# Two vector subtracts moved to GpSimd and a split copy moved to ScalarE in a two-layer diffusion backbone

## The chip, the cores and the metric

The kernel runs on one core of a Trainium2 chip. The metric is device time in microseconds (us) of one execution; lower is better. The engines are named as in the profile: PE is TensorE (PEld its weight loads), DVE is VectorE, ACT is ScalarE, POOL is GpSimd and SP is SyncE, which here only issues transfers.

## The reference, cut to what matters

Two layers work on 512 latent and 256 context tokens of width 1024. All arithmetic is fp32.

```python
for l in range(DEPTH):                                    # DEPTH = 2
    mod = split(silu_c @ w_mod[l] + b_mod[l], 6)          # shift, scale, gate, twice
    p = split_proj((layer_norm(x) * (1 + scale) + shift) @ w_in[l] + b_in[l])
    y_r, y_a, y_m = retention(p), attention(p), mlstm(p)  # three token mixers
    z = sig(g_r) * (y_r @ w_r) + sig(g_a) * (y_a @ w_a) + sig(g_m) * (y_m @ w_m)
    x = layer_norm(alpha * x + mod[2] * (z @ w_o)) * ln1_g + ln1_b
    h = layer_norm(x) * (1 + mod[4]) + mod[3]
    u = depthwise_conv3(h @ w_up[l]) + conv_b[l]
    a, g = split(u, 2)
    x = layer_norm(alpha * x + mod[5] * ((silu(g) * a) @ w_down[l])) * ln2_g + ln2_b
```

The context stream goes through the same steps, except that it is not carried beyond the mixers in the second layer.

## The kernel before, in words

**Split products.** An fp32 matrix product is made of three reduced-precision ones. Each operand is split into a high half (the value rounded to fp32r) and a low half (the value less the high half), and high times high, high times low and low times high are added up in PSUM. So each weight and each activation needs a cast (high half) and a subtract (low half) before PE can use it.

**Weights.** All weights stream from HBM once, mostly in blocks of 128x1024 words. `wblock` (L308) loads a block into `raw` (five buffers, issued by SP), casts it to `wh` on ACT (L313, two buffers) and subtracts to `wl` on DVE (L314, two buffers). There are 358 such blocks. `fm` (L432) uses a block as the stationary operand against the transposed activations `xh` and `xl`; `tm` (L447) uses it as the moving operand. Both first run all products with `wh` and then those with `wl`, so `wl` is needed later than `wh`. Some blocks of the last down-projection are kept for several passes and are split by code of their own (`keep`), with the subtract on DVE.

**Activations.** `to_xT` (L409) takes one token tile of 128 rows that is already normalised, transposes it on PE into PSUM in two halves of 512 columns, copies each 128x128 piece out with the scale and shift of the modulation into `mod`, casts that to `xh` on ACT (L425) and subtracts to `xl` on DVE (L426). The scaled copies of one half run on DVE (L421) and those of the other half on ACT (L423), turn about by tile. There are 88 copies on each engine.

**Layer boundaries.** `finish` (L1049) closes each sub-layer tile by tile: statistics, a power for the reciprocal deviation on POOL (L398), two DVE passes over the tile (L1070, L1071), a square with row sums on ACT (L1080), a second power on POOL (L1083), the bias `nb` on DVE (L1084), the normalised tile `xn` on ACT (L1086), and then `to_xT`. The layer norm at the start (L1031) also ends in `to_xT`.

**Merge operand.** `yprep` (L1294) reads the mixers' outputs back from DRAM into `stg`, casts to `xh` on ACT (L1299) and subtracts to `xl` on DVE (L1300), four pieces for each of two mixers and each layer.

**What sets the order.** The order of PE's instructions is written by hand: a `Mixer` interleaves a foreground generator (projections, merge, FFN) with background ones (mixers, `finish`), by an estimated running time. Every other engine runs in the order that the tile scheduler chose from its own simulation at build time. `wblock` raises the priority of its cast and subtract. Each engine runs its list strictly in order, so an instruction that waits holds back all that stand behind it.

Of the kernel before, what the change touches and what calls it, by code (L numbers as in the profile page):

```python
# [9 lines left out]
F32 = mybir.dt.float32  # L10
F32R = mybir.dt.float32r
BF = mybir.dt.bfloat16
AF = mybir.ActivationFunctionType
OP = mybir.AluOpType
# [189 lines left out]
def _program(es, nc, tc, I, OUT):  # L204
    V, S, G, SP = nc.vector, nc.scalar, nc.gpsimd, nc.sync
# [10 lines left out]
    def tr(out, in_):  # L216
        M.cost(0.107)
        nc.tensor.transpose(out, in_, ident)  # L218
# [12 lines left out]
    def Ht(name="h", dt=F32):  # L231
        return sp.tile([128, 512], dt, name=name, tag="H", bufs=12)
# [4 lines left out]
    def stg(name="stg"):  # L237
        return wp.tile([128, 768], F32, name=name, tag="stg", bufs=3)
# [4 lines left out]
    def pt(name="p"):  # L243
        return psp.tile([128, 512], F32, name=name, tag="p")
# [57 lines left out]
    def wload(src, n=1024):  # L302
        raw = wp.tile([128, 1024], F32, name="raw", tag="raw", bufs=5)
        with tc.high_priority():
            M.wdma = SP.dma_start(out=raw[:, :n], in_=src)
        return raw

    def wblock(src, n=1024):  # L308
        raw = wload(src, n)
        h = wp.tile([128, 1024], F32R, name="wh", tag="wh", bufs=2)  # L310
        l = wp.tile([128, 1024], F32R, name="wl", tag="wl", bufs=2)
        with tc.high_priority():
            S.copy(h[:, :n], raw[:, :n])  # L313
            V.tensor_tensor(l[:, :n], raw[:, :n], h[:, :n].bitcast(F32), op=OP.subtract)  # L314
        return h, l

    mod_tail = []
# [91 lines left out]
    def to_xT(xn, t, xh, xl, mc, sidx, s, hfs=(0, 1)):  # L409
        cols = slice(128 * t, 128 * t + 128)  # L410
        for hf in hfs:
            p = pt("ptr")
            for k in range(4):
                tr(p[:, 128 * k:128 * k + 128], xn[hf][:, 128 * k:128 * k + 128])
            m = Ht("mod")
            for k in range(4):
                kk = 4 * hf + k
                o, i = m[:, 128 * k:128 * k + 128], p[:, 128 * k:128 * k + 128]
                a, b = mc[:, sidx + 1, kk, s:s + 1], mc[:, sidx, kk, s:s + 1]
                if (hf + t) % 2 == 0:  # L420
                    V.tensor_scalar(o, i, a, b, op0=OP.mult, op1=OP.add)  # L421
                else:
                    S.activation(o, i, AF.Identity, scale=a, bias=b)  # L423
            m3 = m.rearrange("p (k t) -> p k t", k=4)
            S.copy(xh[:, 4 * hf:4 * hf + 4, cols], m3)  # L425
            M.xl = V.tensor_tensor(xl[:, 4 * hf:4 * hf + 4, cols], m3, xh[:, 4 * hf:4 * hf + 4, cols].bitcast(F32),  # L426
                                   op=OP.subtract)

    def new_xT():
        return (xp.tile([128, 8, 768], F32R, name="xh", tag="xh"), xp.tile([128, 8, 768], F32R, name="xl", tag="xl"))  # L430
# [16 lines left out]
    def tm(srcs, lhs, tiles, nks, evac, hook=None, w=256):  # L447
        per = 512 // w
        banks = [tiles[i:i + per] for i in range(0, len(tiles), per)]
        gs = [None] * len(banks)  # L450
        tot = sum(nks)
        done = 0
        for src, nk in zip(srcs, nks):
            h, l = src() if callable(src) else wblock(src, nk * w)
            for bi, ts in enumerate(banks):
                if hook:
                    yield from hook(int(done > 0), ts)
                if done == 0:
                    gs[bi] = gt()
                for i, t in enumerate(ts):  # L460
                    for k, pi in [(k, pi) for k in range(nk) for pi in (0, 1)] + [(k, 2) for k in range(nk)]:
                        mm(gs[bi][:, w * i:w * i + w], lhs(done + k, t, pi == 1), (l if pi == 2 else h)[:, w * k:w * k + w],
                           start=(done + k == 0 and pi == 0 and i == 0),
                           stop=(done + k == tot - 1 and pi == 2), skip_group_check=True)
                    yield
                if done + nk == tot:
                    evac(ts, gs[bi][:, :w * len(ts)].rearrange("p (t c) -> p t c", c=w))
            done += nk
# [546 lines left out]
    def start_x(xh, xl):  # L1015
# [22 lines left out]
        for hf in range(2):  # L1038
            if hf:
                yield "mods"  # L1040
            for t in order:
                to_xT(xts[t], t, xh, xl, modc[0], 0, int(t >= 4), (hf,))
                M.done.add(f"x0.0.{t}.{hf}")
                if not hf and t == 4:
                    load(3)
                    norm(3)
                yield 0 if hf else 0.5

    def finish(key, X, xslot, gname, bname, l, tiles, emit, xT=None, mc=None, sidx=0, mi=None):  # L1049
# [3 lines left out]
        def post(t, xn):  # L1053
            need_mod(*mi[:2])
            tmod(*mi[2:])
            to_xT(xn, t, xT[0], xT[1], mc, sidx, int(t >= 4))
            M.done.add(f"{key}.{t}")
# [55 lines left out]
    def layer(l, xT, key):  # L1113
        last = l == DEPTH - 1
        nq = 512 if last else 768
# [104 lines left out]
        for i in range(2):  # L1220
            t = km_[i]
            km.append(t)
            if i:
                gl = []
                for a, b in ALL:
                    p = pt("pgl")
                    for c in range(a, b, 128):
                        tr(p[:, c - a:c - a + 128], glt[:, c:c + 128])
                    gl.append((p[:, :b - a], a, b))
                M.add(mlstm(l, mlstm_rows(gl, bfm), qm, km, vm, chunks, nq))  # L1230
            yield from fm(wblock(I["wfm"][l, B_KM - 1 + i]), xh, xl, ALL,
                          lambda g, a, b: evac_bias(t[:, a:b], g, bq[:, B_KM + i:B_KM + i + 1], scale=0.125))
        for i in range(2):
            t = qm_[i]
            qm.append(t)
            yield from fm(wblock(I["wfm"][l, B_QM - 1 + i]), xh, xl, qseg,
                          lambda g, a, b: evac_bias(t[:, a:b], g, bfm[:, B_QM + i:B_QM + i + 1]))
# [54 lines left out]
        yh, yl = new_xT()  # L1292

        def yprep(bi):  # L1294
            for k in range(4):
                t = stg()
                kk = 4 * (bi % 2) + k
                SP.dma_start(out=t[:, :nq].rearrange("p (c t) -> p c t", t=128), in_=dr_y[bi][:, :nqt, k, :])
                S.copy(yh[:, kk, :nq], t[:, :nq])  # L1299
                V.tensor_tensor(yl[:, kk, :nq], t[:, :nq], yh[:, kk, :nq].bitcast(F32), op=OP.subtract)  # L1300

        def yatt(t, y):
            c = slice(128 * t, 128 * t + 128)
# [23 lines left out]
        def merge(bi, segs):  # L1327
# [3 lines left out]
            for q in range(4):  # L1331
                blk = wblock(I["wbr"][l, bi, q])
                if bi == 0 and q == 1:
                    yprep(1)
# [37 lines left out]
        yold = []  # L1372
        yield f"r{l}"
        yprep(0)
        tmod(0, 4, 4)
        yield from merge(0, qseg)
# [38 lines left out]
        for gr, (go, gnum) in enumerate(zip(GOFF, GROUPS)):  # L1415
# [4 lines left out]
            for pi, segs in enumerate(passes):  # L1420
# [3 lines left out]
                for jn, j in enumerate(range(go, go + gnum)):  # L1424
# [3 lines left out]
                    for half, jj in enumerate((j, NF + j)):  # L1428
                        t = stg("tc")
# [92 lines left out]
```

## Time and profile before

| what | value |
|---|---|
| median of 3 runs | 2539.36 us (2532.22 to 2539.62) |
| the profiled execution: its own time | 2537.32 us |
| its span, first to last instruction | 2535.4 us |
| granted PE clock, mean | 0.987 |
| PE busy | 2430.9 us (96%) |
| DVE busy | 1585.1 us (63%) |
| ACT busy | 1003.1 us (40%) |
| POOL busy | 92.2 us (4%) |

The engines run side by side, so busy times don't add up to the span. A PE that is busy 96% of the time leaves about 104 us of the span in which no matmul ran; the stretches in which these lie are where the other engines matter. The granted clock is the PE clock as a share of full speed: at 1.00 a stretch ran at the upper of two levels (2.4 GHz), at 0.5 at the lower (1.2 GHz), and a mean between them says how much of the stretch was spent at each.

### The profile page before, as it was taken

How to read it: one execution, taken by the hardware profiler on the slowest of the kernel's cores; microseconds unless marked ns; L12 is line 12 of the kernel's file. 1: busy time of each engine (PE TensorE's matmuls, PEld its weight loads, DVE VectorE, ACT ScalarE, POOL GpSimd, SP SyncE). 2: the span in 40 equal slices, each digit the busy share in tenths (PEclk: the TensorE clock that was granted, in tenths of full speed). 3: DMA queues.
4: the chain of work that ended last, by engine and by line, in shares of the span. 5: the costliest groups of instructions: out<-in, count | busy, mean ns of one | idle time of the engine just before them, and what ended most of it. 6: DMA issues, size and time to landing. Idle time of an engine off the chain costs nothing. (4 is left out here: it accounts for less than half of the span.)

```text
span 2535.4 us, 41733 instructions
## 1 busy us (share of the span) xinstructions
PE 2430.9 (96%) x16552; PEld 2147.9 (85%) x16552; DVE 1585.1 (63%) x3338; ACT 1003.1 (40%) x1802; POOL 92.2 (4%) x111
## 2 busy tenths in 40 slices
PE   6999999999899989999999989999999988999998
PEld 4977998888788978999898878779787888988887
DVE  5556465545576885555545773767565877865557
ACT  4423322455433463232313353334254555633332
POOL 1000001000000000000000010000110000000000
PEclk9999999999999999999999999999999999999999
DMA  7344524322545562212121384254434444533232
GB/s 256 103 166 132 164 96 140 105 82 86 188 152 171 193 228 82 82 46 82 55 71 59 114 286 142 94 160 144 160 135 129 140 146 156 183 105 100 84 105 70
DMA packets 147650, 329.20 MB, mean 130 GB/s; under 512 B 15872, under 2 KB 59136, under 8 KB 147456
## 3 DMA queue, kind: packets, MB, share of 16 engines
q1 hardware_dynamic: 147456, 326.54, 39.3%
q8 instruction: 131, 2.15, 0.3%
q14 instruction: 63, 0.52, 0.1%
HBM read 283.49 MB, written 42.99 MB: 129 GB/s over the span
## 5 line engine op out<-in xcount | busy, mean ns | idle before, releaser
L214 PE MATMUL g<-xh,wh 128*128 128x512 f32 (+1 forms) x2448 | 827.4, 353 | 14.7 <-ACT xh L1299 5.4
L214 PE MATMUL g<-xl,wh 128*128 128x512 f32 (+1 forms) x2448 | 814.3, 348 | 5.0 <-DVE xl L426 4.3
L314 DVE TENSOR_TENSOR wl<-raw,wh 128x1024 fp32r<-128x1024 f32 (+3 forms) x358 | 411.8, 1150 | 357.1 <-ACT wh L313 267.7
L313 ACT CAST wh<-raw 128x1024 fp32r<-128x1024 f32 (+3 forms) x358 | 355.4, 993 | 643.1 <-PE g L214 566.4
L214 PEld LDWEIGHTS g<-xh,wh 128*128 128x128 f32 x2448 | 466.6, 191 | 83.2 <-issue 12.4
L214 PEld LDWEIGHTS g<-xl,wh 128*128 128x128 f32 x2448 | 467.3, 191 | 61.8 <-DVE xl L426 4.8
L214 PE MATMUL g<-xh,wl 128*128 128x512 f32 (+1 forms) x2448 | 511.0, 347 | 2.9 <-DVE wl L314 2.9
L214 PEld LDWEIGHTS g<-xh,wl 128*128 128x128 f32 x2448 | 401.8, 190 | 61.3 <-DVE wl L314 3.5
L214 PE MATMUL g<-wh,ah 128*128 128x256 f32 x808 | 205.4, 282 | 4.6 <-ACT ah L1443 3.5
L214 PE MATMUL g<-wh,al 128*128 128x256 f32 x808 | 204.1, 281 | 2.7 <-DVE al L1444 2.7
L214 PE MATMUL g<-wh,xh 128*128 128x256 f32 (+1 forms) x768 | 200.9, 292 | 4.5 <-ACT wh L313 3.3
L214 PE MATMUL g<-wh,xl 128*128 128x256 f32 (+1 forms) x768 | 196.8, 287 | 4.0 <-DVE xl L426 2.4
L214 PEld LDWEIGHTS g<-wh,ah 128*128 128x128 f32 x808 | 151.9, 188 | 6.3 <-ACT ah L1443 4.2
L214 PEld LDWEIGHTS g<-wh,xh 128*128 128x128 f32 x768 | 148.9, 194 | 9.1 <-ACT wh L313 3.8
L214 PEld LDWEIGHTS g<-wh,al 128*128 128x128 f32 x808 | 152.0, 188 | 4.1 <-DVE al L1444 3.5
L214 PEld LDWEIGHTS g<-wh,xl 128*128 128x128 f32 x768 | 149.0, 194 | 5.1 <-DVE xl L426 3.0
L1404 ACT ACTIVATE tc<-g,conv 128x512 f32<-128x512 f32 (+1 forms) x142 | 96.9, 682 | 134.4 <-PE g L214 134.0
L214 PE MATMUL g<-wl,ah 128*128 128x256 f32 x808 | 143.8, 281 | 0.1
L1405 DVE SCALAR_TENSOR_TENSOR tc<-g,conv,tc 128x511 f32<-128x511 f32 (+1 forms) x142 | 88.7, 625 | 83.9 <-ACT tc L1404 83.1
L931 ACT ACTIVATE Pe<-psc,mx 128x256 f32<-128x256 f32 (+1 forms) x144 | 80.6, 565 | 146.1 <-DVE mx L926 100.8
L398 POOL TENSOR_TENSOR rstd<-veps,mhalf 128x1 f32<-128x1 f32 (+3 forms) x68 | 71.2, 1048 | 1801.1 <-DVE veps L396 1789.6
L214 PE MATMUL g<-wl,xh 128*128 128x256 f32 (+1 forms) x768 | 127.9, 287 | 1.0 <-DVE wl L314 0.9
(279 smaller groups left out, 3166.8 us busy)
## 6 DMA issues: line engine op xcount, KB each, us to landing
raw<-in_wup_dram SPq DMA_DIRECT2D x108, 512.0 KB, 3.5
raw<-in_wmod_dram SPq DMA_DIRECT2D x96, 512.0 KB, 5.2
raw<-in_wfm_dram SPq DMA_DIRECT2D x80, 512.0 KB, 3.5
raw<-in_wtm_dram SPq DMA_DIRECT2D x32, 512.0 KB, 4.7
raw<-in_wout_dram SPq DMA_DIRECT2D x32, 512.0 KB, 3.6
raw<-in_wbr_dram SPq DMA_DIRECT2D x28, 512.0 KB, 4.0
dr_g<-stg SPq DMA_DIRECT2D x48, 256.0 KB, 2.0
raw<-in_wdn_dram SPq DMA_DIRECT2D x20, 512.0 KB, 3.6
```

Source lines behind the costliest of these rows:

```text
L214: nc.tensor.matmul(out, lhsT, rhs, **kw)
L313: S.copy(h[:, :n], raw[:, :n])
L314: V.tensor_tensor(l[:, :n], raw[:, :n], h[:, :n].bitcast(F32), op=OP.subtract)
L398: G.tensor_tensor(r, t, mhalf[:, :n], op=OP.pow)
L931: S.activation(pe[:, a:b], prs[si][:, :b - a], AF.Exp, bias=mx[:, 3:4], scale=0.125, accum_out=sm[:, si:si + 1])
L1404: S.activation(t[:, a:b], g, AF.Identity, bias=conv[:, jj, 3:4], scale=conv[:, jj, 1:2])
L1405: V.scalar_tensor_tensor(t[:, a + 1:b], g[:, :b - a - 1], conv[:, jj, 0:1], t[:, a + 1:b], op0=OP.mult, op1=OP.add)
```

## The change

Three statements change. The subtract of every weight block goes from DVE to POOL, the subtract of the merge operand goes from DVE to POOL, and the scaled copies in `to_xT` all go to ACT.

```diff
@@ wblock
         with tc.high_priority():
             S.copy(h[:, :n], raw[:, :n])
-            V.tensor_tensor(l[:, :n], raw[:, :n], h[:, :n].bitcast(F32), op=OP.subtract)
+            G.tensor_tensor(l[:, :n], raw[:, :n], h[:, :n].bitcast(F32), op=OP.subtract)
@@ to_xT
-                if (hf + t) % 2 == 0:
-                    V.tensor_scalar(o, i, a, b, op0=OP.mult, op1=OP.add)
-                else:
-                    S.activation(o, i, AF.Identity, scale=a, bias=b)
+                S.activation(o, i, AF.Identity, scale=a, bias=b)
@@ yprep
                 S.copy(yh[:, kk, :nq], t[:, :nq])
-                V.tensor_tensor(yl[:, kk, :nq], t[:, :nq], yh[:, kk, :nq].bitcast(F32), op=OP.subtract)
+                G.tensor_tensor(yl[:, kk, :nq], t[:, :nq], yh[:, kk, :nq].bitcast(F32), op=OP.subtract)
```

PE's order stays as it is. The scheduler makes new lists for the other engines. Lines behind L421 have numbers lower by 3 in the changed kernel (L423 becomes L420, L425 L422, L426 L423, L1083 L1080).

The first place is ACT at the start, where the first normalised tiles are transposed and scaled. `xt` is a normalised tile, `ptr` the transposed one in PSUM, and `x4` counts equal rows in a run. Before:

```order
L1031 ACTIVATE xt<-xt,nb,rstd 128x512 x6
L345 COPY part<-pp 128x256
L423 ACTIVATE mod<-ptr,modc_83 128x128 x4
L425 CAST xh<-mod 128x4x128 x3
L423 ACTIVATE mod<-ptr,modc_83 128x128 x4
L425 CAST xh<-mod 128x4x128
L1031 ACTIVATE xt<-xt,nb,rstd 128x512 x2
L313 CAST wh<-raw 128x1024
```

And now:

```order
L1028 ACTIVATE xt<-xt,nb,rstd 128x512 x6
L345 COPY part<-pp 128x256
L420 ACTIVATE mod<-ptr,modc_83 128x128 x8
L422 CAST xh<-mod 128x4x128 x2
L420 ACTIVATE mod<-ptr,modc_83 128x128 x4
L1028 ACTIVATE xt<-xt,nb,rstd 128x512 x2
L422 CAST xh<-mod 128x4x128
L420 ACTIVATE mod<-ptr,modc_83 128x128 x4
L313 CAST wh<-raw 128x1024
```

Eight scaled copies now stand ahead of the first cast where four stood, and the last tile's normalisation stands behind twelve copies where it stood behind eight.

The second place is POOL from the end of the first layer's mixers on, where `finish` closes the first sub-layer's tiles. The powers are the `rstd` rows. Before:

```order
L398 TENSOR_TENSOR rstd<-veps,mhalf 128x8 x6
L398 TENSOR_TENSOR rstd<-veps,mhalf 128x1
L1083 TENSOR_TENSOR rstd<-veps,mhalf 128x1
L398 TENSOR_TENSOR rstd<-veps,mhalf 128x1
L1083 TENSOR_TENSOR rstd<-veps,mhalf 128x1
```

And now:

```order
L398 TENSOR_TENSOR rstd<-veps,mhalf 128x8
L314 TENSOR_TENSOR wl<-raw,wh 128x1024 x19
L398 TENSOR_TENSOR rstd<-veps,mhalf 128x1
L314 TENSOR_TENSOR wl<-raw,wh 128x1024
L1080 TENSOR_TENSOR rstd<-veps,mhalf 128x1
L398 TENSOR_TENSOR rstd<-veps,mhalf 128x1
L314 TENSOR_TENSOR wl<-raw,wh 128x1024
L1080 TENSOR_TENSOR rstd<-veps,mhalf 128x1
L314 TENSOR_TENSOR wl<-raw,wh 128x1024
L398 TENSOR_TENSOR rstd<-veps,mhalf 128x1
```

POOL held nothing but the powers there; now weight subtracts stand among them, each between two powers, and neither kind can pass the other.

The third place is DVE in the same boundary, over one tile of `finish`. Before:

```order
L1066 BN_AGGR mv<-bst 128x2
L314 TENSOR_TENSOR wl<-raw,wh 128x1024
L396 TENSOR_SCALAR veps<-mv 128x1
L1070 SCALAR_TENSOR_TENSOR xres<-xres,mv,lnrow 128x512 x2
L348 TENSOR_TENSOR part<-pp,part 128x256
L421 TENSOR_SCALAR mod<-ptr,modc_83 128x128 x4
L1071 SCALAR_TENSOR_TENSOR xres,lnsum<-xres,rstd,lnrow 128x512 x2
L426 TENSOR_TENSOR xl<-mod,xh 128x4x128 x2
L1077 TENSOR_SCALAR nm<-lnsum 128x1
L314 TENSOR_TENSOR wl<-raw,wh 128x1024
```

And now:

```order
L1063 BN_AGGR mv<-bst 128x2
L1100 TENSOR_TENSOR stg<-g,grow 128x512
L396 TENSOR_SCALAR veps<-mv 128x1
L1067 SCALAR_TENSOR_TENSOR xres<-xres,mv,lnrow 128x512 x2
L423 TENSOR_TENSOR xl<-mod,xh 128x4x128
L1102 SCALAR_TENSOR_TENSOR xres<-xres,stg 128x2x256
L1100 TENSOR_TENSOR stg<-g,grow 128x256
L1068 SCALAR_TENSOR_TENSOR xres,lnsum<-xres,rstd,lnrow 128x512 x2
```

The weight subtracts and the four scaled copies are gone from the tile's chain, and accumulations of the next product (L1100, L1102) have moved up into it.

## Rows read from the trace of the kernel before

**Rows 1.** The page's first part: busy time, share and instructions of each engine.

```profile
PE 2430.9 (96%) x16552; PEld 2147.9 (85%) x16552; DVE 1585.1 (63%) x3338; ACT 1003.1 (40%) x1802; POOL 92.2 (4%) x111
```

**Rows 2.** Busy time by stretch at the three boundaries: stretch, us, PE, PEld, DVE, ACT, POOL, clock, DMA.

```profile
900.00:950.00 50.00, 45.04 (x324) 39.26 (x325) 41.56 (x88) 33.16 (x61) 2.74 (x4) 0.93 0.64 222
1450.00:1500.00 50.00, 41.10 (x390) 34.82 (x388) 43.72 (x113) 28.32 (x54) 7.09 (x8) 0.99 0.84 288
1500.00:1550.00 50.00, 46.40 (x375) 43.12 (x376) 26.64 (x60) 20.54 (x39) 5.76 (x12) 0.91 0.59 206
2100.00:2150.00 50.00, 44.22 (x350) 41.70 (x349) 39.18 (x80) 25.20 (x43) 2.13 (x3) 0.93 0.53 180
...
sum 300.00, PE 270.64 PEld 246.12 DVE 241.29 ACT 175.12 POOL 25.25; mean PE 45.11 PEld 41.02 DVE 40.21 ACT 29.19 POOL 4.21
```

**Rows 3.** The same six stretches, L314 alone.

```profile
sum 300.00, DVE 75.47; mean DVE 12.58
```

**Rows 4.** The same six stretches, L421 alone.

```profile
sum 300.00, DVE 21.87; mean DVE 3.65
```

**Rows 5.** PE's waits: what for, us in total, times, longest us.

```profile
PE ptr L218 <- ACT xn L1086: 11.0, 5, 4.8
...
PE g L214 <- DVE xl L426: 6.7, 4, 3.2
...
PE g L214 <- DVE wl L314: 3.9, 2, 2.9
```

**Rows 6.** Groups of instructions by line: shapes, count, busy us, mean ns, idle before.

```profile
L314 DVE TENSOR_TENSOR wl<-raw,wh 128x1024 fp32r<-128x1024 f32 (+3 forms) x358 | 411.8, 1150 | 357.1 <-ACT wh L313 267.7 <-PE g L214 85.2 <-DMA df<-in_cst_dram 1.5
...
L423 ACT ACTIVATE mod<-ptr,modc 128x128 f32<-128x128 f32 x88 | 33.1, 457 | 8.5 <-PE ptr L218 8.5
...
L609 POOL MEMSET aa<- 128x768 f32 x2 | 1.5, 744 | 108.0 <-DVE xx L576 108.0
...
L1300 DVE TENSOR_TENSOR xl<-stg,xh 128x512 fp32r<-128x512 f32 x8 | 5.5, 690 | 8.8 <-ACT xh L1299 8.8
```

**Rows 7.** Timeline, POOL and DVE at two powers: start us, us, instruction, idle before.

```profile
1815.74 0.69 POOL L398 TENSOR_TENSOR rstd<-veps,mhalf 128x2 f32<-128x2 f32 x1 [3.91 <-DVE veps L396]
1815.81 1.23 DVE L314 TENSOR_TENSOR wl<-raw,wh 128x1024 fp32r<-128x1024 f32 x1 [0.15 <-PE g L214]
...
1843.70 1.23 DVE L314 TENSOR_TENSOR wl<-raw,wh 128x1024 fp32r<-128x1024 f32 x1
1843.93 1.55 POOL L398 TENSOR_TENSOR rstd<-veps,mhalf 128x2 f32<-128x2 f32 x1 [3.69 <-DVE veps L396]
```

**Rows 8.** Timeline, weight subtracts and the first matmul that reads them.

```profile
1460.53 1.22 DVE L314 TENSOR_TENSOR wl<-raw,wh 128x1024 fp32r<-128x1024 f32 x1
1461.81 0.73 PE L214 MATMUL g<-wl,ah 128*128 128x256 f32 x4
...
1527.95 1.23 DVE L314 TENSOR_TENSOR wl<-raw,wh 128x1024 fp32r<-128x1024 f32 x1 [0.67 <-ACT wh L313]
1529.24 1.08 PE L214 MATMUL g<-wl,xh 128*128 128x256 f32 x4
```

**Rows 9.** A subtract behind the mLSTM recurrence: timeline, and its stretch.

```profile
1605.16 1.21 DVE L314 TENSOR_TENSOR wl<-raw,wh 128x1024 fp32r<-128x1024 f32 x1
1606.42 2.52 PE L214 MATMUL g<-xh,wl 128*128 128x512 f32 x8 [2.94 <-DVE wl L314]
...
1600.00:1650.00 50.00, 47.06 (x246) 38.95 (x244) 32.31 (x77) 22.37 (x41) 0.00 (x0) 0.93 0.32 100
```

**Rows 10.** Timeline of the start: scaled copies of the second halves on ACT and DVE.

```profile
48.02 2.90 ACT L423 ACTIVATE mod<-ptr,modc 128x128 f32<-128x128 f32 x8 [1.74 <-PE ptr L218]
48.45 3.92 DVE L421 TENSOR_SCALAR mod<-ptr,modc 128x128 f32<-128x128 f32 x12 [1.27 <-PE ptr L218]
```

**Rows 11.** Timeline, weight subtracts in the third boundary.

```profile
2178.14 1.22 DVE L314 TENSOR_TENSOR wl<-raw,wh 128x1024 fp32r<-128x1024 f32 x1 [0.51 <-ACT wh L313]
2181.02 1.23 DVE L314 TENSOR_TENSOR wl<-raw,wh 128x1024 fp32r<-128x1024 f32 x1 [0.28 <-ACT wh L313]
```

## The prediction

> **What bounds the kernel now.** I read the page's busy times first: PE is busy for 2430.9 us, 96% of the span, while DVE has 63%, ACT 40% and POOL 4% [rows 1]. PE's order does not change, so its 2430.9 us stay. What can change is the 104 us of the span without a matmul and the time that PE works at less than its full clock. Next I cut the span into stretches. In the long feed-forward stretches PE has no idle time, so who makes a low half there does not matter as long as it comes in time. The idle time lies at the start, where the modulation weights stream in, and at three boundaries: the end of layer 0's first sub-layer, the change to layer 1, and the end of layer 1's first sub-layer. Six stretches of 50 us cover these three [rows 2]. PE is busy for 270.64 of their 300 us, so 29.4 us are idle, and the granted clock is short of 1.00 by 0.07, 0.01, 0.09 and 0.07 in four of them, which is 0.24 x 50 = 12 us at most. So 41 us are at stake there, and in them DVE is busy for 241 of 300 us, ACT for 175 and POOL for 25 [rows 2]. DVE is the engine in short supply, and that is the case for this change: 75.5 us of weight subtracts [rows 3] and 21.9 us of scaled copies [rows 4] leave it there. The list of PE's waits says what comes last: the normalised tile from ACT (11.0 us), the low half of a tile from DVE (6.7) and a weight's low half (3.9) [rows 5].
>
> **Price of a subtract on POOL.** No row shows one. On DVE it takes 1.22 us for 1024 words per partition [rows 8]. POOL's nearest row is a fill of 768 words in 0.744 us [rows 6]; scaled to 1024 words that is 0.99 us, the lower end, if two reads cost nothing over one write. The upper end is three such passes, 2.98 us, if the two reads and the write go one after the other. I take two passes, 1.98 plus 0.1 for starting, 2.07 us, since the reads have to share something with the write or with each other on an engine that is otherwise never seen to be fast. The Trainium skill ("GPSIMD Engine Reference", section 3.1) gives 4497 ns for 2048 fp32 words against 2293 ns on VectorE; that would be an estimated 2.25 us here, and would add about 1 us to the sum.
>
> The two engines also get in each other's way. A power on POOL took 1.55 us when it was issued 0.23 us after a subtract with two SBUF inputs had started on DVE, and it ended 0.55 us after that subtract; the same power took 0.69 us when it was issued first, and the subtract behind it kept its 1.23 us [rows 7]. So a POOL instruction waits for a running DVE instruction of that kind. Whether DVE waits for a POOL subtract of 2 us isn't shown by any row, since the power reads only two words per partition; the bounds are nothing and the whole 2.07 us. I count 0.35 us for the subtract's own wait, half a DVE instruction of 0.7 us, so a low half comes about 2.4 us after its high half, 1.2 us later than now.
>
> **Part by part**, against the profiled execution of 2537.3 us, which lies 2.1 us under the median of 2539.4.
>
> *Weight subtracts where there is time.* Of 358 low halves [rows 6] PE's matmuls wait for two, 3.9 us in all [rows 5]; outside the places below I take the others to have the 1.2 us to spare, because each block's products with the high half come first and cover them. That cover is gone if POOL needs more time than a block lasts on PE: in the third boundary subtracts follow each other at 2.88 us [rows 11], so 2.4 us still fit and the upper end of 2.98 us does not. Taken: 0.
>
> *Weight subtracts that are just in time.* At four places in the second boundary, from 1460.53 to 1527.95 us, PE's first matmul with the low half starts 0.06 us after the subtract ends [rows 8]. Each is 1.2 us later, 4.8 us, and three neighbours where the low half is also among the last things to arrive make it +6. Lower end: at 0.99 us each a gain of 0.25, so -1. Upper end: seven places at 2 us each and two falls of the clock at 3 us, +20.
>
> *The subtract behind the mLSTM recurrence.* At 1605.16 us a subtract runs last in a row of small DVE instructions and PE waits 2.94 us for it; the clock of its stretch is 0.93, a loss of 3.5 us [rows 9]. POOL is idle there, so both go: -6, between -6.4 and 0 (if the list on POOL puts it behind a power that waits for DVE).
>
> *Scaled copies on ACT.* At the start DVE does 12 copies in 3.92 us while ACT does 8 in 2.90 us [rows 10]; ACT now does them in turn. The first cast stands behind four copies more, 1.45 us; the second halves come up to 12 x 0.36 = 4.4 us later. PE has nothing else to do there. Taken: +4, between 1.4 and 5.8. At the boundaries a tile's two halves no longer go side by side: four copies at 0.36 us are 1.45 us more before the last `xl`, and the next tile's square and `xn`, also on ACT, stand behind them. PE waits for `xn` at five tiles [rows 5], so +7, between 0 (if ACT's idle 125 us [rows 2] take them) and 13 (nine such waits, with the four for `xl` [rows 5]).
>
> *Powers behind subtracts.* The six stretches hold about 64 subtracts (75.5 us [rows 3] at 1.15 to 1.22 us each [rows 6, 8]), 132 us of POOL at 2.07 us each, 44% of the time. A power that finds one under way waits 1.0 us on the mean. Two powers a tile make 0.9 us, at five tiles +4, between 0 and 8. The reverse, a subtract behind a power that waits for DVE, is within the +20 above.
>
> *Merge operand.* Four pieces in turn are paced by their loads; only the last one shows, at 1.5 us on POOL for 0.69 us on DVE [rows 6]: +1, between 0 and 4.
>
> *Relief of DVE.* 97.4 of its 241 us go from the boundaries [rows 3, 4]. If DVE alone made the 41 us, half of them, 20 us, might come back. But POOL streams for 132 us there, and if DVE's two-input passes (the tile passes, `xl`, the sums of row statistics) stop for even half of that, 66 of the 97 us are taken back. Taken: -4, between -20 and +35.
>
> Sum: 4 + 6 + 7 + 4 + 1 - 6 - 4 = +12, so 2549 us.
>
> **Rivals.** *Relief wins.* If a POOL subtract doesn't stop DVE, the boundary chains lose their queueing on DVE: -20, and -6 at the mLSTM place, against +4 at the start and +6 for tight low halves, with the copies and powers hidden: -16, 2521 us. For it speaks DVE's 80% at the boundaries [rows 2] and the unhurt subtract of 1.23 us beside a power [rows 7]; against it, that PE's largest boundary wait is for ACT's `xn` and not for DVE [rows 5]. It decides if a subtract holds DVE for under about 0.3 us.
>
> *It cancels.* ACT takes the copies in its idle time and powers seldom meet a subtract: start +2, tight places +3, copies +3, powers +1, against -6 and -1: +2, 2539 us. For it: each term is a few us, of either sign.
>
> *The lock works both ways.* Each POOL subtract stops DVE's two-input work for its whole length: 132 us of stops for 97 us of relief, +35, with +4 and +6 and -6: +39, 2576 us. It decides from about 1.5 us of stopped DVE per subtract (64 x 1.5 = 96). For it speaks the power that was held up by DVE [rows 7], which is one direction of it; against it, that much of DVE's work at the boundaries reads PSUM, or may run in the 59 us that DVE has idle [rows 2]. The Trainium skill ("SBUF — State Buffer", section "Who interferes with whom") states it as a rule: a VectorE instruction with two SBUF inputs and a GpSimd one that reads SBUF take an exclusive lock, and whichever comes second is fully blocked. By that rule this rival's time would hold; the trace agrees for a GpSimd instruction that comes second (1.55 against 0.69 us), and shows nothing of a VectorE one.
>
> **How the numbers follow.** Chances: the forecast 0.42 (its own range 2547 to 2563), relief 0.26, cancelling 0.22, the lock both ways 0.10. About 0.3% is what a measurement of this kernel can tell from no change, that is 2531.7 to 2547.0 around the median. So faster has 0.26, same 0.22, slower 0.42 + 0.10 = 0.52. For 8 in 10 the range leaves out the better half of the relief case and the worse half of the lock case: 2519 to 2580.
>
> **What would show it.** Right: POOL busy near 358 x 2 = 700 us or more, a subtract of 1.9 to 2.5 us and longer ones where DVE runs tile passes; PE waits for `wl` from POOL in the second boundary, of about 1 us each; DVE's L1070 and L1071 stretched at the boundaries; the wait at 1606 us gone; the first cast of the start 1.5 us later. Wrong: DVE instructions with unchanged times at the boundaries and PE's waits for `xn` shorter (relief), a subtract of about 1 us (the tight places cost nothing), or a subtract near 3 us, with which the blocks of 2.88 us become POOL's pace and the range's upper end is too low.

## The result and the profile after

The changed kernel takes 2595.68 us (median of 4 runs, 2592.75 to 2602.8) against 2539.49 us of the kernel before in the same session: 56 us more, a ratio of 1.0222 with a 95% interval of 1.0201 to 1.0242. The forecast was 2549 us with a range up to 2580. The profiled execution took 2602.8 us, with a span of 2601.0 us.

The page's first part of the changed kernel, which answers to [rows 1]:

```profile
PE 2460.9 (95%) x16552; PEld 2166.3 (83%) x16552; DVE 1414.3 (54%) x2876; ACT 1029.7 (40%) x1890; POOL 933.9 (36%) x485
```

PE was busy for 30 us longer than before with the same instructions (2460.9 against 2430.9 us), and its mean granted clock was 0.979 where it had been 0.987, so a part of the loss stands in no list of waits.

DVE lost 462 instructions: 358 weight subtracts, 88 scaled copies and 16 merge subtracts. By their groups over the whole span ([rows 6] has the first) these were 411.8 + 29.9 + 13.2 = 455 us of its 1585.1 us. That would leave about 1130 us, and it was busy for 1414. So DVE got slower at the work it kept, though its busy time fell. The groups of DVE instructions show where (line, operation, shapes, count, busy us, mean ns, idle before); first the changed kernel, with POOL's new group:

```profile
L1102 DVE SCALAR_TENSOR_TENSOR xres<-xres,stg 128x512 f32<-128x512 f32 x52 | 62.1, 1194 | 1.8 <-DMA xres<-in_ctx_dram 0.4
L423 DVE TENSOR_TENSOR xl<-mod,xh 128x512 fp32r<-128x512 f32 x44 | 48.7, 1123 | 21.5 <-ACT xh L422 21.4
L1081 DVE SCALAR_TENSOR_TENSOR nb<-nm,rstd 128x1 f32<-128x1 f32 x16 | 9.8, 613 | 3.5 <-POOL rstd L1080 3.4
L1100 DVE TENSOR_TENSOR stg<-g,grow 128x512 f32<-128x512 f32 x88 | 60.4, 686 | 147.2 <-PE g L214 147.2
...
L314 POOL TENSOR_TENSOR wl<-raw,wh 128x1024 fp32r<-128x1024 f32 x297 | 724.1, 2441 | 1168.3 <-ACT wh L313 963.8 <-PE g L214 184.5 <-ACT xh L1357 8.5
```

The same groups of the kernel before:

```profile
L1105 DVE SCALAR_TENSOR_TENSOR xres<-xres,stg 128x512 f32<-128x512 f32 x52 | 35.5, 687 | 1.5 <-DMA xres<-in_ctx_dram 0.9
L426 DVE TENSOR_TENSOR xl<-mod,xh 128x512 fp32r<-128x512 f32 x44 | 29.4, 682 | 2.8 <-ACT xh L425 2.8
L1084 DVE SCALAR_TENSOR_TENSOR nb<-nm,rstd 128x1 f32<-128x1 f32 x16 | 2.5, 154 | 1.5 <-POOL rstd L1083 1.4
L1103 DVE TENSOR_TENSOR stg<-g,grow 128x512 f32<-128x512 f32 x88 | 60.6, 689 | 22.6 <-PE g L214 22.4
```

The first three read two operands from SBUF and take 1.7, 1.6 and 4 times as long. The fourth, of the same size as the first, takes one operand from PSUM and keeps its 0.69 us. Summed over all DVE instructions as duration less the mean of the same line and shape before, the kept instructions grew by 250 us, and 176 of them are over 0.3 us longer than their like. (Instructions overlap at their ends, so this sum and the 284 us of busy time are not the same.) Of the 176, 154 read two operands from SBUF; the other 22 scale a tile from SBUF to SBUF by per-partition scalars. The timeline of the first boundary shows one of them (start us, us, instruction, idle before):

```profile
944.30 2.37 POOL L314 TENSOR_TENSOR wl<-raw,wh 128x1024 fp32r<-128x1024 f32 x1
...
944.37 2.32 DVE L1081 SCALAR_TENSOR_TENSOR nb<-nm,rstd 128x1 f32<-128x1 f32 x1 [0.66 <-POOL rstd L1080]
...
946.78 1.52 ACT L1083 ACTIVATE xn<-xres,nb,rstd 128x512 f32<-128x512 f32 x2 [2.42 <-DVE nb L1081]
```

A DVE instruction on one word per partition started 0.07 us behind a POOL subtract and ended with it, at 946.69 against 946.67 us; the normalised tile on ACT waited for it. So DVE is held up for the whole rest of the subtract. It is no single case: all 57 of the L1102 instructions that began with more than 0.5 us of a POOL subtract to go were lengthened, to 0.55 us (512 columns) or 0.28 us (256) past its end, and none of the 37 L1100 that began so. The prediction had this as its third rival, with a chance of 0.10.

PE's waits (what for, us, times, longest), to be held against [rows 5]:

```profile
PE g L214 <- ACT wh L313: 21.1, 11, 6.6
...
PE g L214 <- POOL wl L314: 16.7, 24, 1.5
PE g L214 <- DVE xl L423: 9.4, 7, 2.8
...
PE ptr L218 <- ACT xn L1083: 3.5, 4, 1.0
```

PE's order is the same in all kernels here, so the n-th of the 16552 matmuls is the same one in each, and its start can be compared. The table gives by how much a kernel fell behind the kernel before (+) or gained on it (-) in each stretch, from the first matmul after the times given, in the profiled executions; the columns are the changed kernel and four of the experiments below. The changed kernel's column adds up to 65.6 us and not to 56, since its profiled execution was the longest of its four.

| stretch, us of before | what | changed | subtracts on POOL | copies on ACT | extra subtracts | two fills |
|---|---|---|---|---|---|---|
| 0 to 150 | start | +14.3 | +3.6 | +7.2 | +9.4 | -0.9 |
| 150 to 800 | layer 0 projections, mixers | -0.8 | +0.4 | -2.5 | +13.1 | -3.6 |
| 800 to 1000 | first boundary | +8.5 | +11.1 | +0.4 | +33.8 | -4.3 |
| 1000 to 1400 | FFN | +0.5 | +0.2 | +0.5 | 0.0 | +0.4 |
| 1400 to 1650 | second boundary, mLSTM start | +15.6 | +20.2 | +1.7 | +21.3 | -8.1 |
| 1650 to 2100 | layer 1 projections, mixers | +13.4 | +10.2 | -1.2 | +28.6 | -3.4 |
| 2100 to 2250 | third boundary | +11.6 | +11.0 | +0.7 | +39.0 | -7.3 |
| 2250 to the end | FFN, last norm | +2.5 | +3.8 | +3.1 | 0.0 | +1.0 |

In these eight stretches the kept DVE instructions of the changed kernel grew by 12, 39, 39, 18, 39, 44, 46 and 13 us. The same 39 us went with no loss in layer 0's mixers and with 8.5 and 15.6 us at the first two boundaries, so the price of a stop goes by the place where it falls. And in the stretches that answer to [rows 2] (865 to 970, 1475 to 1587 and 2151 to 2262 us) DVE was busy for less than before, 234.6 us against 241.29, while they took 328 us for 300:

```profile
sum 328.00, PE 279.55 PEld 249.84 DVE 234.60 ACT 194.56 POOL 173.12; mean PE 46.59 PEld 41.64 DVE 39.10 ACT 32.43 POOL 28.85
```

Two places differ from what the list of waits suggests. At the start, ACT's list now runs sixteen copies in one go while PE waits for the cast behind them:

```profile
53.31 5.69 ACT L420 ACTIVATE mod<-ptr,modc 128x128 f32<-128x128 f32 x16 [1.98 <-PE ptr L218]
58.80 0.70 ACT L422 CAST xh<-mod 128x512 fp32r<-128x512 f32 x1
...
59.56 0.58 PE L214 MATMUL g<-wh,xh 128*128 128x256 f32 x1 [2.61 <-ACT xh L422]
```

Before, ACT and DVE shared these [rows 10]. The clock fell with it: from 60 to 90 us the mean granted clock is 0.84, where it was 1.00.

```profile
60.00:90.00 30.00, 28.75 (x202) 28.31 (x202) 8.67 (x21) 10.20 (x19) 10.49 (x6) 0.84 0.32 97
```

At the mLSTM mixer of layer 1 PE's wait for the low half [rows 9] is gone, and a longer one for a high half stands in its place:

```profile
1619.03 2.39 POOL L314 TENSOR_TENSOR wl<-raw,wh 128x1024 fp32r<-128x1024 f32 x1
...
1619.16 2.53 DVE L581 TENSOR_TENSOR_SCAN bb<-ones,xx 4x128 f32<-4x128 f32 x1
...
1639.25 0.84 ACT L605 ACTIVATE li<-li 36x768 f32<-36x768 f32 x1 [13.64 <-DVE li L604]
1640.00 1.03 ACT L313 CAST wh<-raw 128x1024 fp32r<-128x1024 f32 x1
...
1641.08 0.79 PE L214 MATMUL g<-xh,wh 128*128 128x512 f32 x1 [6.62 <-ACT wh L313]
```

Two of DVE's scans took 2.5 us for 0.41 because of POOL subtracts, and ACT's list has the cast of the next weight block behind an activation that waits for DVE's recurrence.

### The profile page after: what moved, and what is told of

Read it like the earlier page. It is cut to its first block, busy times and chain, and to the rows that moved or that the text cites. A ratio compares the mean times of both kernels' runs of the same rounds, so it can differ in the third digit from the quotient of the medians.

```text
span 2601.0 us, 41795 instructions
## 1 busy us (share of the span) xinstructions
PE 2460.9 (95%) x16552; PEld 2166.3 (83%) x16552; DVE 1414.3 (54%) x2876; ACT 1029.7 (40%) x1890; POOL 933.9 (36%) x485
## 3 DMA queue, kind: packets, MB, share of 16 engines
q8 instruction: 131, 2.15, 0.3%
## 5 line engine op out<-in xcount | busy, mean ns | idle before, releaser
L314 POOL TENSOR_TENSOR wl<-raw,wh 128x1024 fp32r<-128x1024 f32 (+3 forms) x358 | 820.2, 2294 | 1352.5 <-ACT wh L313 1102.7
L1100 DVE TENSOR_TENSOR stg<-g,grow 128x512 f32<-128x512 f32 (+1 forms) x112 | 70.3, 629 | 148.8 <-PE g L214 148.7
```

What stands on the lines that cost most here:

```text
L314: G.tensor_tensor(l[:, :n], raw[:, :n], h[:, :n].bitcast(F32), op=OP.subtract)
L1100: V.tensor_tensor(t3, g[:, i:i + n], bc(rows[int(t >= 4)][hf][:, 256 * co:256 * co + 256], 1, n), op=OP.mult)
```

## The experiments

The theory after the result: a POOL subtract that reads SBUF stops DVE's instructions with two SBUF operands for its whole length, and that makes the loss. The rivals: the copies on ACT make it, the low halves come too late, or POOL's strict order does. Times are medians of one session; each kernel is compared with the kernel before in its own session.

| kernel | us | before | ratio, 95% interval |
|---|---|---|---|
| weight subtracts alone on POOL | 2597.5 | 2540.7 | 1.0234 (1.0217 to 1.0251) |
| scaled copies alone on ACT | 2542.8 | 2540.7 | 1.0010 (0.9998 to 1.0022) |
| before, with an extra subtract on POOL | 2683.1 | 2540.7 | 1.0565 (1.0546 to 1.0583) |
| two fills on POOL in place of the subtract | 2510.5 | 2540.7 | 0.9882 (0.9866 to 0.9899) |
| three fills on POOL | 2533.5 | 2542.4 | 0.9965 (0.9950 to 0.9980) |
| FFN up-projection's subtracts on POOL | 2552.9 | 2542.4 | 1.0044 (1.0031 to 1.0058) |
| merge operand alone on POOL | 2531.0 | 2542.4 | 0.9961 (0.9945 to 0.9976) |
| one subtract on POOL | 2541.4 | 2542.4 | 0.9999 (0.9986 to 1.0013) |
| two copies on POOL in place of the subtract | 2655.3 | 2541.0 | 1.0455 (1.0436 to 1.0474) |
| the change without its weight subtracts | 2542.7 | 2541.0 | 1.0014 (1.0000 to 1.0027) |

**Which part makes the loss.** First the weight subtracts alone, then the copies alone:

```diff
@@ wblock
-            V.tensor_tensor(l[:, :n], raw[:, :n], h[:, :n].bitcast(F32), op=OP.subtract)
+            G.tensor_tensor(l[:, :n], raw[:, :n], h[:, :n].bitcast(F32), op=OP.subtract)
```

> Only the weight subtracts go to POOL. Theory (lock): the DVE instructions with two SBUF inputs are stretched by some 250 us in all, as in the changed kernel, and the time is 35 to 50 us over the kernel before; the start is unchanged. Rival (the copies on ACT did most of it): under 20 us over.

```diff
@@ to_xT
-                if (hf + t) % 2 == 0:
-                    V.tensor_scalar(o, i, a, b, op0=OP.mult, op1=OP.add)
-                else:
-                    S.activation(o, i, AF.Identity, scale=a, bias=b)
+                S.activation(o, i, AF.Identity, scale=a, bias=b)
```

> Only the scaled copies go to ACT. Theory: the start loses its 12 to 14 us, the rest moves by a few us either way, so 10 to 18 us over the kernel before. Rival (copies cost the boundaries most): 30 us or more over, with PE waits for xn longer.

The subtracts alone cost 57 us, as much as the whole change and more than the 35 to 50 expected, and DVE's kept instructions grew by 250 us, as in the changed kernel; the start, expected unchanged, lost 3.6 us. The copies alone cost 2 us, below what was expected, and a difference that the interval doesn't tell from none; the profiled execution shows their 7.2 us at the start, and at most 3.1 us of either sign in any later stretch. The change without its weight subtracts (copies on ACT, merge operand on POOL) is the other half of the test:

> The change without its weight subtracts: scaled copies on ACT and the merge operand on POOL. Theory (the weight subtracts make all of the loss): within 8 us of the kernel before, of either sign, since the two parts alone gave 2 over and 11 under. Rival (the parts cost together what they don't cost alone): 15 us or more over.

It came out 1.7 us over, so nothing of the 56 us is left without the weight subtracts.

**Holding up DVE, or late low halves?** The kernel before kept its subtract on DVE and got a second one on POOL that nobody waits for:

```diff
@@ wblock
             V.tensor_tensor(l[:, :n], raw[:, :n], h[:, :n].bitcast(F32), op=OP.subtract)
+            G.tensor_tensor(raw[:, :n], raw[:, :n], h[:, :n].bitcast(F32), op=OP.subtract)
```

> The kernel before, with a second subtract of the same size on POOL behind each weight subtract on DVE, whose result nobody reads (it overwrites the raw block, which is dead by then). The low halves are in time. Theory (lock): DVE's two-input instructions are stretched as in the changed kernel, and the time is 30 to 60 us over the kernel before. Rival (low halves late, or stuck between powers on POOL): 0 to 10 us over, from powers behind the extra subtracts alone.

It lost 142 us, more than twice the upper end. DVE's instructions grew by 307 us with no work taken off it, and its own weight subtracts are among those that grew, which then come late:

```profile
L314 DVE TENSOR_TENSOR wl<-raw,wh 128x1024 fp32r<-128x1024 f32 x297 | 396.4, 1335 | 220.8 <-ACT wh L313 163.6 <-PE g L214 50.0 <-DMA raw<-in_wbr_dram 2.1
```

```profile
PE g L214 <- DVE wl L314: 25.7, 21, 3.6
PE ptr L218 <- ACT xn L1087: 17.7, 9, 6.4
```

No low half was made on POOL here, so its slower subtract is not needed for a loss. This kernel doesn't rule out POOL's order, since the powers still stand between subtracts there, and the extra subtract also keeps the raw block's buffer for longer. The counter-test leaves the place and nearly the length of the POOL work and takes away the reading:

```diff
@@ wblock
-            V.tensor_tensor(l[:, :n], raw[:, :n], h[:, :n].bitcast(F32), op=OP.subtract)
+            G.tensor_tensor(l[:, :2], raw[:, :2], h[:, :2].bitcast(F32), op=OP.subtract)
+            for _ in range(2):
+                G.memset(l[:, :n].bitcast(F32), 0.0)
```

> The weight subtracts stand on POOL as in the changed kernel, but each is a subtract of 2 words and two fills of the whole block with zeros, about 2.1 us that read nothing from SBUF; the low halves of the weights are left out. Copies and merge operand as before. Theory (lock, by reading): DVE's instructions keep their times of before, PE still waits for low halves at the just-in-time places, and the time is between 8 us under and 12 us over the kernel before. Rival (late low halves and order on POOL): 30 us or more over, like the weight subtracts alone.

It gained 30 us, far more than the lower end, and DVE's two-operand groups are back at their old durations (line numbers are 2 higher here):

```profile
L1107 DVE SCALAR_TENSOR_TENSOR xres<-xres,stg 128x512 f32<-128x512 f32 x52 | 35.9, 691 | 2.3 <-DMA xres<-in_ctx_dram 0.9
L428 DVE TENSOR_TENSOR xl<-mod,xh 128x512 fp32r<-128x512 f32 x44 | 29.9, 687 | 9.6 <-ACT xh L427 9.3
```

```profile
L316 POOL MEMSET wl<- 128x1024 f32 x594 | 568.7, 958 | 33.6
L314 POOL TENSOR_TENSOR wl<-raw,wh 128x2 fp32r<-128x2 f32 x358 | 84.0, 234 | 1414.8 <-ACT wh L313 1276.0 <-ACT ah L1445 64.1 <-issue 27.6
```

So 412 us of weight subtracts fewer on DVE are worth 30 us if next to nothing comes back in their place (22 us did, 18 of them in one other kind of instruction, see the last section). POOL's order is nearly that of the weight subtracts alone, and makes no loss here. The fills also let go of the raw block earlier, behind 2 words, so that a load can start sooner; that is worth little, as far as waits show: PE's waits for high halves whose cast stood behind a load come to 8.5 us with the weight subtracts alone, 3.4 with two fills and 4.4 in the kernel before. These POOL stretches are 0.234 + 2 x 0.958 = 2.15 us, 0.29 us shorter than the subtract's 2.44. A third fill goes past it, to 3.11 us:

```diff
-            for _ in range(2):
+            for _ in range(3):
```

> Like the kernel with two fills, but with three, so that a low half is ready about 3.1 us after its high half, later than the 2.4 us of the real subtract, and still nothing of size is read on POOL; the low halves of the weights are left out. Theory (reading holds DVE up): the kernel stays 0 to 25 us under the kernel before, with more PE waits for low halves than with two fills. Rival (late low halves make the loss): 25 us or more over.

It is still 9 us under the kernel before, and PE now waits where the prediction had looked for late low halves:

```profile
PE g L214 <- POOL wl L316: 24.5, 25, 3.4
```

Against 7.9 us at 8 places with two fills. So lateness costs 0.83% of the time, 21 us, for 0.96 us. At the subtract's 2.44 us that would be, by proportion, some 6 us of loss against two fills, and the move without its reading would have gained about 24 us. Measured is a loss of 57, so the reading costs about 81 us. The 81 is an estimate from three measured kernels and lets the cost of lateness grow evenly with time; its sign and order are shown by the two fill kernels alone, which lie on both sides of the subtract's length and are both under the kernel before.

**Is one operand enough?** The fills became copies of the raw block:

```diff
-                G.memset(l[:, :n].bitcast(F32), 0.0)
+                G.tensor_copy(l[:, :n], raw[:, :n])
```

> Like the kernel with two fills, but each fill is a copy of the whole raw block on POOL, so that the two passes read one SBUF operand as well as write one; the low halves of the weights are left out (copies of the block stand in their place). Theory (reading holds DVE up, one operand is enough): two-input DVE instructions are stretched again by 100 us or more, and the time is 20 us or more over the kernel before. Rival (only two operands read at once do it): DVE's two-input instructions keep their times and the time stays 10 to 35 us under the kernel before.

DVE's instructions grew by 114 us and 158 of them by over 0.3 us. Of the `xl` subtracts in `to_xT` all 13 that began with more than 0.5 us of a copy to go were lengthened, and with two fills none of the 7 that began so, so one operand read on POOL is enough to hold DVE up. The 114 us of time are not a clean price: the scheduler drew the copies of different blocks into one another on POOL, and PE waited for low halves for most of it.

```profile
PE g L214 <- POOL wl L316: 95.1, 55, 11.2
```

**Where it counts.** Only the 108 subtracts of the up-projection went to POOL:

```diff
-                        yield from fm(wblock(I["wup"][l, jj]), hh, hl, segs,
+                        yield from fm(wblock(I["wup"][l, jj], eng=True), hh, hl, segs,
```

> Only the 108 weight subtracts of the feed-forward up-projection go to POOL, 30% of the 358. Theory (a held-up DVE costs only where PE is waiting for DVE): 0 to 6 us over the kernel before, although DVE's instructions are stretched there too. Rival (the loss goes by the number of subtracts): 30% of 57, about 17 us over.

It lost 10 us, between the two. By pairs of matmuls it lost 6.5 us between 900 and 950 us and 6.1 between 2100 and 2200, where the first up-projections run beside the tiles of `finish`, 1.5 at the end, and 0.0 from 950 to 1450, although DVE's instructions grew by 8 us between 1000 and 1400. (It lost 2.2 us between 650 and 800 too, where none of its subtracts stand.) So neither the number of subtracts nor the stretch of DVE (57 us) sets the price, but whether PE waits for DVE just then. The theory's place was right, its amount too small: the up-projection reaches into the boundaries.

**The merge operand alone:**

```diff
@@ yprep
-                V.tensor_tensor(yl[:, kk, :nq], t[:, :nq], yh[:, kk, :nq].bitcast(F32), op=OP.subtract)
+                G.tensor_tensor(yl[:, kk, :nq], t[:, :nq], yh[:, kk, :nq].bitcast(F32), op=OP.subtract)
```

> Only the merge operand's 16 subtracts go to POOL. Theory: 0 to 3 us over the kernel before. Rival: nothing at all, since the loads set the pace.

A miss for both: it gained 11 us, and is the fastest of the kernels here that compute the whole result, 0.4% under the kernel before and 2.5% under the changed one. Of its 7 us in the profiled execution 2.4 came near the merge operand of layer 0 (690 to 700 us) and 5.0 between 930 and 940 us, 240 us behind it. There the kernel before has a PE wait for a tile's low half, behind four products for the gate rows on DVE:

```profile
932.01 2.49 DVE L373 TENSOR_TENSOR dg<-ident,modc 128x512 f32<-128x512 f32 x4
...
934.82 0.68 DVE L426 TENSOR_TENSOR xl<-mod,xh 128x512 fp32r<-128x512 f32 x1
...
935.55 0.79 PE L214 MATMUL g<-xl,wh 128*128 128x512 f32 x1 [3.16 <-DVE xl L426]
```

With the merge operand on POOL the scheduler's list has both low halves ahead of those products:

```profile
926.99 0.68 DVE L426 TENSOR_TENSOR xl<-mod,xh 128x512 fp32r<-128x512 f32 x1
...
929.02 0.69 DVE L426 TENSOR_TENSOR xl<-mod,xh 128x512 fp32r<-128x512 f32 x1
929.62 2.49 DVE L373 TENSOR_TENSOR dg<-ident,modc 128x512 f32<-128x512 f32 x4
```

So much of its gain looks like another order that the scheduler happened to choose, and not the 16 subtracts. The change without its weight subtracts has the same 16 on POOL, gains 0.9 us at that place, and is no faster than the kernel before. That was read from the traces and not tried by itself. If it is right, lists alone can move this kernel by some 5 us at one place.

**One subtract,** the one that PE waited for at 1606.42 us [rows 9]:

```diff
-            V.tensor_tensor(l[:, :n], raw[:, :n], h[:, :n].bitcast(F32), op=OP.subtract)
+            (G if M.nb == 201 else V).tensor_tensor(l[:, :n], raw[:, :n], h[:, :n].bitcast(F32), op=OP.subtract)
```

> One weight subtract alone goes to POOL, the one at 1605.16 us of the kernel before, which stood last behind the recurrence of the mLSTM mixer. Theory: PE's wait of 2.94 us and the fall of the clock after it go, 4 to 7 us under the kernel before. Rival (its place is taken by a high half that stands behind the same recurrence on ACT): within 2 us of the kernel before.

No difference, but not by the rival's way. The wait of 2.94 us went, and one of 1.70 us came at the block before it, whose subtract is still on DVE and stands behind the same recurrence; that was itself held up by the one subtract on POOL (a sum of 4 words that takes 0.14 us elsewhere took 2.10):

```profile
1597.45 2.57 POOL L315 TENSOR_TENSOR wl<-raw,wh 128x1024 fp32r<-128x1024 f32 x1 [10.06 <-PE g L214]
...
1597.93 2.10 DVE L605 TENSOR_TENSOR mp<-bb,mm 4x1 f32<-4x1 f32 x1
```

## Why the prediction was wrong

The direction was right, the amount was not: +12 us forecast, +56 measured, outside the range.

- **The step that failed is "Relief of DVE", -4.** It set the time for which POOL stops DVE against the time that DVE is relieved of, and took the kernel to gain by the balance. As DVE time it came near. In the stretches of the boundaries DVE's kept instructions grew by 78 us, about half of the 148 us of POOL subtracts there, where the prediction took half of 132, 66 us; against that stand the 97 us that left. So a balance in favour of DVE was left, and yet the three boundaries lost 35.7 us, where the terms for them add up to +7 with this one. A stop lengthens whatever two-operand work DVE begins just then. At the boundaries that can be a link of the chain, like the one-word `nb` that held the normalised tile for 2.3 us, while PE had waited for only two of the 358 low halves that left DVE [rows 5].

  The relief by itself was there, at the term's lower end of -20: with two fills the same three stretches gained 19.7 us (the mLSTM place included) and the whole program 30. POOL's reading cost about 81 us in the whole program, an estimate; relief, stops and late low halves together lost 57 us with the weight subtracts alone, where the term's upper end was +35. The prediction had seen that a running DVE instruction delays POOL [rows 7], and had no row for the other direction.
- **The third rival was right on the stop and wrong on its price.** It set 132 us of stops against 97 of relief, and asked for 1.5 us of stopped DVE per subtract. Measured at the boundaries are 78 us for 62 subtracts, 1.3 us each, which is less than the relief; by its own sum it would not have come true. That its +39 is the nearest of the forecasts is partly luck: it priced a balance too, and the three boundaries only, where layer 1's projections and mixers lost 13.4 us as well. The Trainium skill's rule ("SBUF — State Buffer", section "Who interferes with whom"), that the one that comes second is fully blocked, holds by this trace: `nb` ended 0.02 us after the subtract, 2.32 us for 0.154.
- **PE's 2430.9 us "stay":** they became 2460.9, at a mean clock of 0.979 for 0.987. No term had this beyond the clock of single places.
- **Price of a subtract:** forecast 2.07 us and 0.35 of waiting, 2.4 in all; measured 2.441 on the mean. The sum is right by luck: the shortest of the 297 took 2.34 us, so the subtract itself takes longer than was forecast and waits less.
- **Low halves in time elsewhere, +6 at the tight places:** PE waits for POOL's low halves at 24 places for 16.7 us, where seven were counted. Too low by about 10.
- **The mLSTM place, -6:** the wait moved to a high half and grew to 6.62 us; its other end, 0, covered only a power in front of the subtract, not the stops of the recurrence itself. The single subtract shows the same on a small scale.
- **Copies at the start, +4:** the start lost 14.3 us. The copies alone lose 7.2 there, above their upper end of 5.8: their list has sixteen of them ahead of a cast too, and the clock of that run was 0.80 from 30 to 35 us and 0.51 from 35 to 40, where it had been 1.00. Subtracts alone lose 3.6. What makes the rest was not tried.
- **Copies at the boundaries, +7:** hardly there; the copies alone moved the three boundaries by +0.4, +1.7 and +0.7 us. PE's wait for `xn` fell from 11.0 [rows 5] to 3.5 us. That is the lower end, by which ACT's idle time takes the copies.
- **Merge operand, +1:** -11 when it moves alone, much of it by a new order of lists as far as the traces show, and no such gain beside the copies.

## What to carry to other kernels

GpSimd was no free second VectorE for elementwise work on SBUF here: a VectorE instruction with two SBUF operands that began while a GpSimd instruction read SBUF ended only after it (`nb`, 2.32 us for 0.154). VectorE's busy time still fell, from 1585 to 1414 us, and the kernel got slower, since time that comes free where nobody waits doesn't pay for stops on the chain. So don't set the one against the other as sums. Before such a move, list what VectorE runs in the stretches where TensorE waits for it. In these runs work with one operand in PSUM was not held up (L1100, 686 ns for 689), and a GpSimd fill left two-operand work alone. Price a relief by a version with the work left out or replaced by something harmless (here 30 us), and where a scheduler makes the lists, reckon with an edit that shuffles them elsewhere, as the 16 merge subtracts seem to have done for 5 us at one place.

## What the runs showed of the hardware

How long a VectorE instruction is held goes by what is left of the GpSimd subtract and not by its own size: 128x1 and 4x1 took 2.32 and 2.10 us behind one. Fills on GpSimd left two-operand instructions alone, but lengthened another kind: scalings from SBUF to SBUF by per-partition scalars, 31 of them by over 0.3 us and 18 us in all. With two fills the 128x128 normalisation from SBUF (L488, L486 before) takes 490 ns instead of 342, and the same one from PSUM stays at 404:

```profile
L488 DVE TENSOR_SCALAR yn<-hs,hmv,rstd 128x128 f32<-128x128 f32 x40 | 14.5, 490 | 6.8 <-POOL rstd L400 6.7
L488 DVE TENSOR_SCALAR yn<-pO,hmv,rstd 128x128 f32<-128x128 f32 x40 | 13.7, 404 | 9.7 <-POOL rstd L400 9.7
```

GpSimd's price by operands read, for 128x1024 words: 0.96 us for a fill, 1.09 for a copy, 2.44 for a subtract, waits for VectorE included.
